# Where TensorE's operands begin within 512 bytes: the experts' and five blocks' stored values moved by some bytes

## The chip, the core and the metric

The kernel runs on one core of a Trainium2 chip. The metric is the device time of one execution in microseconds, lower is better; the median of three runs is given, and one more execution was taken with the hardware profiler.

## The reference

Two transformer blocks follow one another over 256 tokens of 1024 features, in float32. The first has four feed-forward parts, two mixers between them and norms; the second has two layers of three mixers each, one feed-forward part and one mixture of eight experts. What the change touches is the feed-forward part (five times) and the experts:

```python
def swiglu(h, w_gate, w_up, w_down):          # 1024 -> 2816 -> 1024
    return (jax.nn.silu(h @ w_gate) * (h @ w_up)) @ w_down

def moe_swiglu(h2, w_router, w_gate, w_up, w_down):
    logits = (h2 @ w_router).astype(jnp.float32)
    top_logits, top_idx = lax.top_k(logits, TOP_K)          # 2 of 8
    top_w = jax.nn.softmax(top_logits, axis=-1)
...
    hid = jax.nn.silu(lax.ragged_dot(xs, w_gate, sizes)) * lax.ragged_dot(xs, w_up, sizes)   # 1024 -> 3584
    y = lax.ragged_dot(hid, w_down, sizes)                                                    # 3584 -> 1024
```

## The kernel before, in words

Every product of a weight matrix is made of three matmuls. A number is split into a high part that the float32r type holds and the rest, and hi·hi, hi·lo and lo·hi are added up in PSUM (`mm3w`, `mm3x`; the matmul itself is line 250). Weights come from HBM as a stream of chunks of 1 MB (`raw`, line 142 on SyncE's queue). ScalarE makes the high part of two pieces of 512 columns at a time (`wh`, line 159), VectorE the rest (`wl`, line 160). Four buffers of each are in turn use, and the next pieces are loaded and split some pieces ahead.

There are two ways to multiply. In `proj_t`, used by the five feed-forward blocks, the weights are the stationary operand (128 columns of `wh` or `wl`) and the activations are streamed, 256 columns at a time. A block's first half streams `xh` and `xl` (1056 matmuls), its second half streams the block's inner values `hh` and `hl` (`ffn_core`; 22 pieces of 128 features by 4 outputs of 256 by 2 by 3, 528 matmuls). In `proj_x` and in the experts it is the other way round: the activations are stationary (128 columns) and the weights are streamed, 512 columns at a time. In `moe`, `gate_up` has the gathered tokens `gxh` and `gxl` as the stationary operand, and `down` has the hidden values `mhh` and `mhl`. `gather` fetches an expert's tokens with a one-hot matrix `P`, which is streamed against `xh` and `xl`; `scatter` streams an expert's result `yhl` against the transposed one-hot matrix `PT`.

In the profile a matmul is named out<-moving,stationary: `pa<-xh,wh` streams `xh` against loaded `wh`. PEld is the loading of the stationary operand; it runs ahead, so that one matmul streams while the next one's operand is loaded.

The blocks run in this order: block 1 (first block's layer 0, first part), the even mixer, blocks 2 and 3, the odd mixer, block 4, the first layer of mixers, block 5 (`ffn2`), the second layer of mixers, the experts.

Tiles are placed by pools, one after the other. `gap(pool, n, name)` (line 178) takes n bytes per partition of a pool and never uses them, so that what follows begins n bytes later. Every slice that a matmul reads begins at a multiple of 512 bytes within its tile, so the byte at which the tile begins, within 512, is that of all its operands. In the built program `wh` and `wl` begin at byte 448, `xh` and `xl` at 128, whatever the gaps.

Of the kernel before, what the change touches and what calls it, by code (L numbers as in the profile page):

```python
# [177 lines left out]
def gap(pool, n, name):  # L178

    pool.tile([128, n // 4], F32, name="gap_" + name)


class Net:
# [1193 lines left out]
        self.ln_finish(self.vec("lnmix", 0, 8), self.vec("lnmix", 8, 8))  # L1379

    def ffn2(self):
        self.ffn_core("ffn_w_gate_2", "ffn_w_up_2", "ffn_w_down_2", (0,), (0,), None, self.residual2, free=128)
        self.ln_finish(self.vec("lnffn", 0, 8), self.vec("lnffn", 8, 8))

    def ln_stats(self, x):
# [56 lines left out]
    def moe(self):  # L1442
        nc, tc, W = self.nc, self.tc, self.wk
        V = nc.vector
        Z = self.mo
        x = self.hx
        C = self.consts(Z, "moe")
        gap(Z, 256, "mo")
        cr = Z.tile([128, 2, 128], F32R, name="cr")
        V.tensor_copy(cr[:, 0], C["before"])  # L1450
        V.tensor_copy(cr[:, 1], self.ones)
# [296 lines left out]
    def run(self):  # L1748
        tc = self.tc
        self.setup()  # L1750
        with tc.tile_pool(name="evw", bufs=1, reuse_waits="tile") as P:
            steps = self.even_loads(P)
            self.ffn1(0, 0, steps, free=352)
            for _ in steps:
                pass
            self.even()
        with tc.tile_pool(name="s5p", bufs=1, reuse_waits="tile") as P2:
            with tc.tile_pool(name="s5q", bufs=1, reuse_waits="tile") as P:
                steps = self.s5_params(P, P2)
                self.ffn1(0, 1, steps, free=128)  # L1760
                self.ffn1(1, 0, steps, free=128)
                for _ in steps:
                    pass
            self.odd()
        self.ffn1(1, 1, after=self.between)
        self.ctx1.close()
        with tc.tile_pool(name="l2", bufs=1, reuse_waits="tile") as Q:
            self.l2 = Q
            gap(Q, 128, "l2")
            self.layer0()  # L1770
        self.ffn2()
        self.run_last()
# [100 lines left out]
```

## Time and profile before

| what | value |
|---|---|
| three runs | 3131.31, 3135.25, 3145.41 us |
| median | 3135.25 us |
| profiled execution | 3134.77 us |
| its span | 3133.0 us |
| TensorE busy in matmuls | 3042.3 us, 97% of the span |
| loading of stationary operands | 2739.8 us, 87% |
| VectorE busy | 2334.4 us, 75% |
| ScalarE busy | 1870.3 us, 60% |
| read from HBM | 691.92 MB |
| mean granted clock of TensorE | 0.989 |

A matmul's duration in the profile runs from its start to the end of its last column and overlaps the next one's, so the busy share of TensorE does not tell its pace. The pace is the time from start to start. A row of the timeline gives starts to 0.01 us (x2 stands for two merged matmuls); a row of the table of stretches gives the number of matmuls that lie in a stretch, those included that began just before it.

### The profile page before, as it was taken

To read this page: it belongs to the slowest core of one execution; us is meant where nothing else is said; L and a number is where in the kernel's file an instruction comes from. 1 tells how busy PE (TensorE), PEld (TensorE's weight loads), DVE (VectorE), ACT (ScalarE), POOL (GpSimd) and SP (SyncE) were. 2 spreads that over 40 slices of the span, in tenths; PEclk is the share of its full clock that TensorE was granted. 3 is DMA by queue.
4 is the path that set the end of the run, shared out by engine and by line. 5 is a ranking of instruction groups with operands and counts; after the bars stand their busy time and mean duration, and the time that the engine had idled before them with its cause. 6 is when DMAs were issued, how large, how long until landed. Compare 5 with 4: busy or idle time off the path is not lost. (4 is left out here: it accounts for less than half of the span.)

```text
span 3133.0 us, 51873 instructions
## 1 busy us (share of the span) xinstructions
PE 3042.3 (97%) x20841; PEld 2739.8 (87%) x20841; DVE 2334.4 (75%) x3444; ACT 1870.3 (60%) x2561; POOL 177.6 (6%) x155
## 2 busy tenths in 40 slices
PE   8999999999999999999999999999999999999998
PEld 8997999995899899899998898987787777877876
DVE  6667787868766675566556765569999888889888
ACT  5456555552453654554546654458787777777775
POOL 1000000002102000112010000000000000000000
PEclk9999999999999999999999999999999999999999
DMA  6542555551455333454553335659998998998993
GB/s 251 199 162 92 180 189 180 198 212 55 167 197 177 134 123 137 170 194 159 192 189 122 122 130 184 239 201 348 349 366 325 352 359 331 358 355 328 359 359 151
DMA packets 97415, 696.38 MB, mean 222 GB/s; under 512 B 10880, under 2 KB 11232, under 8 KB 13456
## 3 DMA queue, kind: packets, MB, share of 16 engines
q1 hardware_dynamic: 95184, 685.81, 59.5%
q0 software_dynamic: 752, 3.85, 0.4%
q8 instruction: 165, 2.70, 0.3%
q10 hardware_dynamic: 1232, 3.34, 0.3%
q14 instruction: 82, 0.67, 0.1%
HBM read 691.92 MB, written 1.05 MB: 221 GB/s over the span
## 5 line engine op out<-in xcount | busy, mean ns | idle before, releaser
L160 DVE TENSOR_TENSOR wl<-raw,wh 128x1024 fp32r<-128x1024 f32 x1299 | 1583.2, 1236 | 491.5 <-ACT wh L159 483.0
L159 ACT ACTIVATE wh<-raw 128x1024 fp32r<-128x1024 f32 x1299 | 1361.7, 1060 | 791.1 <-PE pa L250 643.7
L250 PE MATMUL pa<-xh,wh 128*128 128x256 f32 x3072 | 864.3, 281 | 12.9 <-ACT wh L159 9.5
L250 PE MATMUL pa<-xl,wh 128*128 128x256 f32 x3072 | 862.4, 281 | 4.0 <-DVE xl L348 3.9
L250 PE MATMUL pa<-xh,wl 128*128 128x256 f32 x3072 | 861.7, 281 | 1.0 <-DVE wl L160 1.0
L250 PEld LDWEIGHTS pa<-xh,wh 128*128 128x128 f32 x3072 | 582.4, 190 | 17.0 <-ACT wh L159 9.5
L250 PEld LDWEIGHTS pa<-xl,wh 128*128 128x128 f32 x3072 | 583.5, 190 | 6.4 <-DVE xl L348 5.0
L250 PEld LDWEIGHTS pa<-xh,wl 128*128 128x128 f32 x3072 | 585.0, 190 | 1.8 <-DVE wl L160 1.5
L250 PE MATMUL pa<-wl,gxh 128*128 128x512 f32 x896 | 354.5, 396 | 1.4 <-DVE wl L160 1.3
L250 PE MATMUL pa<-wh,gxl 128*128 128x512 f32 x896 | 353.9, 395 | 0.0
L250 PE MATMUL pa<-wh,gxh 128*128 128x512 f32 x896 | 322.5, 395 | 0.0
L250 PE MATMUL pa<-hh,wl 128*128 128x256 f32 x880 | 245.5, 279 | 0.0
L250 PE MATMUL pa<-hl,wh 128*128 128x256 f32 x880 | 245.5, 279 | 0.0
L250 PE MATMUL pa<-hh,wh 128*128 128x256 f32 x880 | 245.3, 279 | 0.0
L250 PEld LDWEIGHTS pa<-wl,gxh 128*128 128x128 f32 x896 | 168.1, 188 | 44.8 <-DVE wl L160 4.1
L250 PEld LDWEIGHTS pa<-wh,gxh 128*128 128x128 f32 x896 | 168.0, 188 | 40.8
L250 PEld LDWEIGHTS pa<-wh,gxl 128*128 128x128 f32 x896 | 168.1, 188 | 40.6
L250 PE MATMUL pb<-wl,mhh 128*128 128x512 f32 x448 | 179.1, 400 | 1.1 <-DVE wl L160 1.1
L250 PE MATMUL pb<-wh,mhl 128*128 128x512 f32 x448 | 177.9, 397 | 0.0
L250 PEld LDWEIGHTS pa<-hh,wl 128*128 128x128 f32 x880 | 166.0, 189 | 0.1
L250 PEld LDWEIGHTS pa<-hl,wh 128*128 128x128 f32 x880 | 165.9, 189 | 0.0
L250 PEld LDWEIGHTS pa<-hh,wh 128*128 128x128 f32 x880 | 165.8, 188 | 0.0
(508 smaller groups left out, 4040.3 us busy)
## 6 DMA issues: line engine op xcount, KB each, us to landing
raw<-in_moe SPq DMA_DIRECT2D x336, 1024.0 KB, 5.7
raw<-in_dense SPq DMA_DIRECT2D x315, 1024.0 KB, 4.8
c_lay<-in_c_lay POOLq DMA_DIRECT2D x2, 1152.0 KB, 7.0
x<-in_xt SPq DMA_DIRECT2D x4, 256.0 KB, 5.7
raw<-in_dense SPq DMA_DIRECT2D x4, 256.0 KB, 6.3
w<-in_cw ACTq DMA_DIRECT2D x1, 1024.0 KB, 8.1
out_dram<-hx SPq DMA_DIRECT2D x2, 512.0 KB, 2.6
c_odd<-in_c_odd POOLq DMA_DIRECT2D x1, 768.0 KB, 4.6
```

Source lines behind the costliest of these rows:

```text
L159: self.nc.scalar.activation(h, src, AF.Copy)
L160: self.nc.vector.tensor_sub(l, src, h)
L250: self.nc.tensor.matmul(out, l, r, start=start, stop=stop, skip_group_check=True)
```

## The change

Six sizes of gaps are altered, one argument is added, and nothing else:

```diff
     def ffn2(self):
-        self.ffn_core("ffn_w_gate_2", "ffn_w_up_2", "ffn_w_down_2", (0,), (0,), None, self.residual2, free=128)
+        self.ffn_core("ffn_w_gate_2", "ffn_w_up_2", "ffn_w_down_2", (0,), (0,), None, self.residual2, free=352)
...
         C = self.consts(Z, "moe")
-        gap(Z, 256, "mo")
+        gap(Z, 448, "mo")
...
             steps = self.even_loads(P)
-            self.ffn1(0, 0, steps, free=352)
+            self.ffn1(0, 0, steps, free=480)
...
                 steps = self.s5_params(P, P2)
-                self.ffn1(0, 1, steps, free=128)
-                self.ffn1(1, 0, steps, free=128)
+                self.ffn1(0, 1, steps, free=384)
+                self.ffn1(1, 0, steps, free=96)
...
-        self.ffn1(1, 1, after=self.between)
+        self.ffn1(1, 1, after=self.between, free=32)
```

Every engine has the same instructions in the same order with the same waits, in both built programs. What moves is where tiles begin, in the built programs' bytes per partition:

| tiles | begin before, within 512 | after, within 512 |
|---|---|---|
| `hh`, `hl` of block 1 | 141952, 128 | 142080, 256 |
| of block 2 | 179840, 128 | 180096, 384 |
| of block 3 | 179840, 128 | 179808, 96 |
| of block 4 | 123008, 128 | 123040, 160 |
| of block 5 | 122496, 128 | 122720, 352 |
| `gxh`; `gxl` has the same byte within 512 | 137472, 256 | 137664, 448 |
| `mhh`, `mhl`, first buffer of three | 153856, 256 | 154048, 448 |
| `P` of the gather | 135424, 256 | 135616, 448 |
| `PT` of the scatter, first buffer of two | 166272, 384 | 166464, 64 |

(For `hh` the first number is that of `hh`; `hl` begins 22528 bytes later, at the same byte within 512.) The small tiles of the experts' pool move by the same 192 bytes. `wh`, `wl`, `xh`, `xl`, `yhl`, the chunks and everything else stay.

## Rows read from the trace of the kernel before

**Rows 1.** Busy time of each engine in stretches, dense part, then experts.

```profile
core 0: us, PE busy (x) PEld busy (x) DVE busy (x) ACT busy (x) POOL busy (x), PEclk, DMA share, GB/s
0.00:220.00 220.00, 209.19 (x1776) 208.20 (x1776) 143.88 (x184) 108.85 (x149) 16.64 (x17) 1.00 0.60 213
220.00:440.00 220.00, 216.86 (x1758) 201.32 (x1757) 170.74 (x448) 128.86 (x260) 9.56 (x6) 0.98 0.41 145
...
2420.00:2640.00 220.00, 217.22 (x970) 174.46 (x969) 197.51 (x190) 170.62 (x192) 0.00 (x0) 1.00 0.92 350
```

**Rows 2.** Waits from 2200 to 3000 us: us in total, times, longest.

```profile
SPq L142 <- DVE wl L160: 673.0, 260, 6.8
...
ACT wh L159 <- DMA raw<-in_moe: 13.4, 40, 0.3
```

**Rows 3.** TensorE in stretches of 256-column matmuls alone: two first halves, six second.

```profile
350.00:440.00 90.00, 90.00 (x766) 1.00 0.53 189
560.00:630.00 70.00, 70.00 (x620) 1.00 0.54 189
140.00:198.00 58.00, 58.00 (x495) 1.00 0.53 183
455.00:512.00 57.00, 57.00 (x487) 1.00 0.53 187
640.00:694.00 54.00, 54.00 (x479) 1.00 0.55 195
980.00:998.00 18.00, 18.00 (x161) 1.00 0.57 180
1578.00:1590.00 12.00, 12.00 (x108) 1.00 0.55 188
1600.00:1637.00 37.00, 37.00 (x317) 1.00 0.53 186
```

**Rows 4.** Timeline of TensorE, experts: first and last of 71 starts.

```profile
2293.66 0.39 PE L250 MATMUL pb<-wh,mhh 128*128 128x512 f32 x1
...
2310.00 0.40 PE L250 MATMUL pb<-wl,mhh 128*128 128x512 f32 x1
```

**Rows 5.** The same, second layer's projections: first and last of 48 starts.

```profile
1908.24 0.39 PE L250 MATMUL pa<-wh,xh 128*128 128x512 f32 x1
...
1919.00 0.39 PE L250 MATMUL pa<-wh,xl 128*128 128x512 f32 x1
```

**Rows 6.** The same, 256 columns of weights streamed: first and last of 39.

```profile
1023.12 0.28 PE L250 MATMUL pa<-wh,xh 128*128 128x256 f32 x1
...
1027.43 0.28 PE L250 MATMUL pa<-wh,xl 128*128 128x256 f32 x1
```

**Rows 7.** The same, the gather, two places.

```profile
2348.25 0.39 PE L250 MATMUL pb<-P,xl 128*128 128x256 f32 x2
...
2348.72 0.40 PE L250 MATMUL pb<-P,xl 128*128 128x256 f32 x2
...
2349.89 0.40 PE L250 MATMUL pb<-P,xh 128*128 128x256 f32 x2
...
2350.61 0.40 PE L250 MATMUL pb<-P,xl 128*128 128x256 f32 x2
```

**Rows 8.** Groups of the page: busy us, mean ns; idle before, releaser.

```profile
L250 PE MATMUL pa<-wl,gxh 128*128 128x512 f32 x896 | 354.5, 396 | 1.4 <-DVE wl L160 1.3
...
L250 PE MATMUL pa<-hh,wl 128*128 128x256 f32 x880 | 245.5, 279 | 0.0
...
L250 PE MATMUL pb<-wl,mhh 128*128 128x512 f32 x448 | 179.1, 400 | 1.1 <-DVE wl L160 1.1
```

**Rows 9.** The experts' stage: its ends, its loads, two stretches of matmuls alone.

```profile
2104.17 0.39 PE L250 MATMUL pa<-wh,gxh 128*128 128x512 f32 x1
...
3116.14 0.40 PE L250 MATMUL pb<-wh,mhl 128*128 128x512 f32 x1
...
raw<-in_moe SPq DMA_DIRECT2D x336, 1024.0 KB, 5.7
...
2264.00:2275.00 11.00, 11.00 (x49) 1.00 1.00 375
2300.00:2308.00 8.00, 8.00 (x36) 1.00 0.98 376
```

## The prediction

> **What bounds the kernel now.** I read the table of stretches first. In the dense part TensorE is busy nearly all the time while DMA stands at 0.41 to 0.60; in the experts TensorE is again busy 217 of 220 us, but DMA stands at 0.92 [rows 1]. The queue's own waits say that the experts' loads are not late: SP waited 673 us of an 800 us stretch for a weight buffer to come free, and the split on ScalarE waited only 13.4 us for data [rows 2]. So TensorE sets the end in both parts, and what matters is its pace: the time from one matmul's start to the next one's.
>
> The pace comes from a timeline (last start less first start, over the steps between) or from a stretch that holds one kind alone (its length plus one duration of 0.28 us, over its count; a missing record or two shifts that by some tenths of a ns). For two matmuls of 256 columns the same instructions on the same bytes run at two levels. In the first block's first half 766 in 90 us are 117.9 ns each, in the third's 620 in 70 us are 113.4 ns [rows 3]. The half that the change touches has both levels too: 495 in 58 us (117.7), 487 in 57 us (117.6), 479 in 54 us (113.3), 161 in 18 us (113.5), and in the fifth block first 108 in 12 us (113.7, that is 113.3 within a record), then 317 in 37 us (117.6) [rows 3]. I call 113.3 and 117.8 the two levels and their difference, 4.4 ns, a step. The clock is granted in full (1.00, that is 2.4 GHz) in all of these.
>
> For the experts' 512 columns there are 70 steps from 2293.66 to 2310.00, 233.4 ns each [rows 4]. The same shape in another place, the second layer's projections with xh and xl as the loaded operand, makes 47 steps from 1908.24 to 1919.00, 228.9 ns each [rows 5]: one step lower.
>
> **What differs between those two places is the byte.** While one matmul streams its moving operand, the stationary operand of the next is loaded. Let D be the byte at which the loaded operand starts less that of the streamed one, within 512. In the blocks D is 448-128 = 320, in the experts 256-448, again 320; in the place of [rows 5] it is 128-448, that is 192. Two smaller places widen this. 256 columns at D = 192 make 38 steps in 1027.43-1023.12 us, 113.4 ns [rows 6]; the gather, at D = 128-256 = 384, makes 6 steps from 2349.89 to 2350.61, 120.0 ns, and elsewhere 4 from 2348.25 to 2348.72, 117.5 ns [rows 7]. So along D = 192, 320, 384 the pace stays or rises: 113.4, then 113.3 or 117.8, then 117.5 to 120.0; and 228.9, then 233.4. That is the whole evidence; no steady run at D = 0, 64, 96, 288 or 352 exists in the trace.
>
> **The change part by part.** No instruction is added, removed or moved, no DMA either, so everything hangs on 4032 expert matmuls (3 x 896 and 3 x 448) and 2640 of the blocks' second half (3 x 880) [rows 8].
>
> Experts: D goes from 320 to 0, which is 512 on a circle of 512. Seen from 384, 0 lies 128 bytes further on in the direction in which the pace rose; seen from 192 it lies 192 bytes back. I take the first, and one step only: 233.3 + 4.4 = 237.8 ns. 4032 x 4.44 ns = **+17.9 us**. Nothing hides it, as TensorE has no slack there. The other ends: one step down, the level of [rows 5], -17.9; two steps either way, 35.8.
>
> The rule that speaks against any effect is dealt with among the rivals.
>
> Blocks, 528 matmuls each, in order of time, with D after: the first (192) goes from 117.8 to the 113.4 of [rows 6], -2.3 us; the second (64, beyond 0 in the rising direction) from 117.8 to 122.2, +2.3 (by the other end -2.3); the third (352, between 320 and 384) from 113.3 to 117.8, +2.3 (or 0); the fourth (288) stays at 113.3, 0 (or +2.3); the fifth (96), now 113.3 for about a quarter and 117.8 for the rest, 116.7, goes to 122.2, +2.9 (or -1.8). Sum **+5.2 us**, ends -6.4 and +9.8.
>
> Gather and scatter: the gather's D goes from 384 to 192, some 96 of its 128 matmuls at full clock by about 6 ns, -0.6 us; the scatter's goes from 256 to 448, 64 matmuls, +0.3 by one step. Together **-0.3 us**. The other tiles that follow in the experts' pool move by 192 bytes too, but feed VectorE and ScalarE, which have slack (197 and 171 of 220 us) [rows 1], and no wait is new.
>
> The sum is 17.9 + 5.2 - 0.3 = +22.8 us on the profiled execution's 3134.8 us: **3157.6 us**, with the 0.5 us by which the median lies above it 3158. Of what is not in the sum: the first halves keep their bytes but may come to stand at the other level after another pause; that is 1056 x 4.44 ns = 4.7 us for each block, of either sign, and three such flips are about what the three runs of before spread (3131 to 3145).
>
> **Rivals.** *Faster: the rise wraps before D = 0.* What returns to its start after 512 bytes must fall somewhere, between 384 and 512 or between 512 and 704 (which is 192). If it falls before 512, the experts stand at the low end: 228.9, -17.9 us, or 224.4, -35.8. The place is the 4032 expert matmuls alone, and it decides as soon as a run of 70 shows a pace under 231 ns. With the blocks at 64 and 96 low as well (-6.4 and less) the time is 3110, or 3093 with two steps. Weights would come fast enough: the stage runs from 2104.17 to 3116.14 us, 1012 us, for 336 chunks of 1024 KB, 352.3 MB, 348 GB/s; 36 us less asks for 361, and stretches without anything else move 375 and 376 GB/s [rows 9]. For it: the share of the circle left for the fall, 320 bytes, of which 128 lie before 512. Against it: nothing between 192 and 384 shows a fall.
>
> *No change: the byte does not matter, or one level stays.* The two levels at equal bytes in [rows 3] show that something other than D sets the pace as well, and the same history could have put [rows 5] one step lower. Then the experts stay at 233.3, the blocks trade a few us and the time is 3135, give or take 7. The Trainium skill, "SBUF — State Buffer", section "Who interferes with whom", gives TensorE two independent read ports, one for the streamed operand and one for the weight load, and says that it never waits on anyone; by that rule D cannot matter and the sum would be 0. The trace agrees only in part: [rows 4] against [rows 5] differ by 4.5 ns per matmul, in dozens of steps each. That the change does not do what it says can be set aside: the built program's addresses are those named above.
>
> *Slower by more.* If the rise goes on at 4.4 ns per 128 bytes from 320, D = 512 costs a step and a half to two: up to +35.8, with the blocks' upper end +9.8, about 3180.
>
> **How the numbers follow.** No change means within 0.5%, 15.7 us, about what a measurement of this kernel can tell. Slower, one step or two: 0.48, since both shapes rise from 192 on. Faster: 0.31, since 128 of 320 bytes would be 0.4, less a little for the two-level spread that favours no step. No change: 0.21. The slower case alone holds 3150 to 3182. The range for 8 in 10 takes in the one-step faster case and its flips, 3102, and the two-step slower one, 3182.
>
> **What would show it.** Right: runs of 70 expert matmuls at 237.8 ns or more, the stage 18 us longer than 2104 to 3116, DMA below 0.92, and the blocks' second halves at 113 in the first and above 118 in the second and fifth. Wrong in the size: 242 ns. Wrong in the sign: 228.9 or less. Wrong in kind: 233.3 unchanged, or levels in the second halves that do not follow D.

## The result, and the profile after

The changed kernel takes 3117.76 us, the median of 12 runs (3104.48 to 3133.01); the kernel before, run beside it, 3138.02 (3123.37 to 3147.78). The ratio is 0.9937 with an interval of 0.9919 to 0.9956: faster by 0.6%, where the prediction said slower. The profiled execution took 3122.09 us, its span is 3120.3 us, 12.7 less than before, at the same mean granted clock of 0.989.

The page after gives the groups that answer to [rows 8] (busy us, mean ns of one | idle before, releaser), and the loads.

```profile
span 3120.3 us, 51873 instructions
...
L250 PE MATMUL pa<-wl,gxh 128*128 128x512 f32 x896 | 349.9, 390 | 1.6 <-DVE wl L160 1.4
...
L250 PE MATMUL pa<-hh,wl 128*128 128x256 f32 x880 | 247.1, 281 | 0.0
...
L250 PE MATMUL pb<-wl,mhh 128*128 128x512 f32 x448 | 177.3, 396 | 1.1 <-DVE wl L160 1.1
...
raw<-in_moe SPq DMA_DIRECT2D x336, 1024.0 KB, 5.7
```

The experts' matmuls went from 396 and 400 ns to 390 and 396, the blocks' from 279 to 281: the two parts of the change moved in opposite directions. The timeline of TensorE after gives the pace: the stage's first and last matmul, and between them the first and last of 71 starts in one run, which answer to [rows 4].

```profile
2113.87 0.39 PE L250 MATMUL pa<-wh,gxh 128*128 128x512 f32 x1
...
2282.76 0.39 PE L250 MATMUL pb<-wh,mhh 128*128 128x512 f32 x1
...
2298.66 0.39 PE L250 MATMUL pb<-wl,mhh 128*128 128x512 f32 x1
...
3103.44 0.39 PE L250 MATMUL pb<-wh,mhl 128*128 128x512 f32 x1
```

70 steps in 15.90 us are 227.1 ns, against 233.4 before. The stage lasts 3103.44 - 2113.87 = 989.6 us, against 1012.0 [rows 9]: **-22.4 us**. But it begins 9.7 us later than the 2104.17 of before. So the dense part lost **+9.7 us**, and -22.4 + 9.7 = -12.7 is the whole of the span's change. Over all its steps the stage divides like this (mean of the steps under 250 ns, and the sum of all steps of the kind):

```
                             before            after
gxh, gxl loaded (2631)   233.3 ns, 616.9 us   226.9 ns, 600.6 us   -16.3
mhh, mhl loaded (1239)   233.2 ns, 294.7 us   228.3 ns, 288.8 us    -5.9
gather, scatter and others         100.4 us            100.2 us     -0.2
```

The table of stretches after, in the places of [rows 1] and [rows 3]: two of the experts, then the second halves of the five blocks in order.

```profile
2200.00:2420.00 220.00, 216.69 (x991) 177.60 (x990) 203.08 (x198) 176.30 (x194) 0.00 (x0) 1.00 0.92 354
2420.00:2640.00 220.00, 217.17 (x991) 178.18 (x990) 201.44 (x195) 174.11 (x195) 0.00 (x0) 1.00 0.94 357
...
134.00:195.00 61.00, 61.00 (x520) 61.00 (x519) 34.04 (x34) 27.50 (x33) 2.76 (x2) 1.00 0.52 184
446.00:506.00 60.00, 60.00 (x512) 60.00 (x511) 41.59 (x67) 30.78 (x41) 2.97 (x2) 1.00 0.53 188
636.00:695.00 59.00, 59.00 (x499) 59.00 (x498) 40.53 (x67) 28.12 (x36) 3.77 (x3) 1.00 0.56 201
962.00:1004.00 42.00, 42.00 (x357) 42.00 (x356) 24.82 (x22) 18.30 (x21) 14.50 (x9) 1.00 0.52 186
1600.00:1643.00 43.00, 43.00 (x369) 43.00 (x368) 24.44 (x21) 17.57 (x18) 9.17 (x6) 1.00 0.53 183
```

In 2420 to 2640 us there are 991 matmuls where there were 970 [rows 1]. DMA went up from 0.92 to 0.94 of its time and from 350 to 357 GB/s, not down: the faster TensorE was fed. The queue's own waits from 2200 to 3000 us after:

```profile
SPq L142 <- DVE wl L160: 670.6, 265, 6.7
```

SyncE's queue still waited 670.6 us for a buffer, against 673.0 [rows 2], so the bound is the same as before.

The blocks' second halves, taken from start to start over the whole half (a stretch's length over its count comes within 1% of it):

```
block   before: D, ns    after: D, ns     said
1       320  117.8       192  117.8       113.4
2       320  117.8        64  117.8       122.2
3       320  113.3       352  118.7       117.8
4       320  113.4       288  118.3       113.3
5       320  116.6        96  117.3       122.2
```

One thing moved whose bytes did not. The place of [rows 5], 512 columns at D = 192, has its 48 starts here after:

```profile
1916.72 0.40 PE L250 MATMUL pa<-wh,xh 128*128 128x512 f32 x1
...
1927.69 0.40 PE L250 MATMUL pa<-wh,xl 128*128 128x512 f32 x1
```

47 steps in 10.97 us are 233.4 ns, where the same instructions on the same bytes took 228.9 before.

### The profile page after: what moved, and what is told of

The parts are those of the page before. It is cut to its first block, busy times and chain, and to the rows that moved or that the text cites. A ratio compares the mean times of both kernels' runs of the same rounds, so it can differ in the third digit from the quotient of the medians.

```text
span 3120.3 us, 51873 instructions
## 1 busy us (share of the span) xinstructions
PE 3029.6 (97%) x20841; PEld 2749.1 (88%) x20841; DVE 2331.8 (75%) x3444; ACT 1869.7 (60%) x2561; POOL 177.9 (6%) x155
```

## The experiments

The prediction's theory was a pace that rises with D in steps of 4.4 ns; its rivals were a fall before D = 0, and a pace that does not depend on D. Two kinds of kernels tell them apart: small ones with nothing but matmuls, and the network with one part of the change.

### m1_sweep: every D in steps of 32 bytes

The network is left out; what is left is this, for 512 columns and then 256, each with d from 0 to 480 in steps of 32, three times over:

```diff
+for i in range(STEPS):
+    g, j = divmod(i, 3)
+    st = (xh, xh, xl)[j]
+    mv = (wh, wl, wh)[j]
+    so = (g % 8) * 128 + d // 4
+    mo = (g % 4) * 256
+    nc.tensor.matmul(o, st[:, so:so + 128], mv[:, mo:mo + cols], start=i == 0, stop=i == STEPS - 1,
+                     skip_group_check=True)
```

> This kernel leaves the whole network out: it runs 60 matmuls in a row of the kernel's float32r form for each distance D = 0, 32, ..., 480 between the loaded and the streamed operand's byte, once with 512 and once with 256 columns, three times over, with a pause for an eviction between runs and no other engine busy. Theory A (the distance sets the pace, and falls back somewhere between 384 and 512): 512 columns show about 229 ns at 192, 233 at 320, 227 at 0, the same in all three repeats, with a fall between 384 and 512; 256 columns show 113 to 118 with a shape of their own. Theory B (history: the level is drawn after each pause, whatever the bytes): the same D gives different levels in the three repeats, for 512 columns as for 256. Theory C (the other engines' traffic makes the difference): all D give one pace here.

The table of stretches shows a quiet chip: no load, no VectorE, the clock granted in full. Columns as in [rows 1].

```profile
375.00:610.00 235.00, 223.27 (x964) 176.98 (x963) 0.00 (x0) 9.35 (x16) 0.00 (x0) 1.00 0.00 0
```

The timeline, in pairs the 13th and the 60th start of a run: D = 0 and 320 with 512 columns, then D = 0 and 64 with 256.

```profile
382.74 0.39 PE L58 MATMUL pa<-wh,xh 128*128 128x512 f32 x1
...
393.39 0.39 PE L58 MATMUL pa<-wh,xl 128*128 128x512 f32 x1
...
531.93 0.39 PE L58 MATMUL pa<-wh,xh 128*128 128x512 f32 x1
...
542.90 0.40 PE L58 MATMUL pa<-wh,xl 128*128 128x512 f32 x1
...
620.38 0.28 PE L58 MATMUL pa<-wh,xh 128*128 128x256 f32 x1
...
626.02 0.28 PE L58 MATMUL pa<-wh,xl 128*128 128x256 f32 x1
...
636.21 0.28 PE L58 MATMUL pa<-wh,xh 128*128 128x256 f32 x1
...
641.54 0.28 PE L58 MATMUL pa<-wh,xl 128*128 128x256 f32 x1
```

47 steps: 226.6, 233.4, 120.0 and 113.4 ns. All of it, worked out in this way:

```
D              0    32    64    96   128   160   192   224
512 columns  226.7 233.3 233.3 234.4 232.4 233.4 228.8 233.3
256 columns  120.0 118.4 113.3 117.4 118.7 120.1 113.3 116.7
```

D = 256 to 480 repeats the same row: 256 gives 226.7 and 120.0, 320 gives 233.3 and 113.3. (Two places differ between the three repeats: 256 columns came out at 117.8, 113.3 and 117.8 at 448, and at 117.7, 116.7 and 117.7 at 480. The rest agrees in all of them, the very first run at a lower clock aside.) So the circle has 256 bytes, not 512; the pace does not rise steadily along it, and at 0 the two widths stand at opposite ends: the lowest for 512 columns, nearly the highest for 256. That settles the experts: D = 0 is one of their best places, and D = 320 the same as 64.

It also settles the rival of no effect. The Trainium skill, "SBUF — State Buffer", section "Who interferes with whom", has two independent read ports for TensorE; here, with no load and no VectorE at work, the distance between the two operands alone is worth up to 7.7 ns per matmul (226.7 against 234.4). The trace does not agree with two reads that are independent.

### m2_absolute: is it D, or the byte itself?

D is held at 0, 192 and 320, and both operands move together by 0 to 448 bytes in steps of 64:

```diff
-    so = (g % 8) * 128 + d // 4
-    mo = (g % 4) * 256
+    so = (g % 8) * 128 + (d + byte) // 4
+    mo = (g % 4) * 256 + byte // 4
```

> The network is left out here too. D is held at 0, 192 and 320 while both operands move together through eight bytes, 64 apart, two repeats. If only the distance counts (theory A), the eight bytes give one pace for each D (512 columns: 227, 229, 233 ns). If the streamed operand's own byte counts, the pace goes through several levels within one D. If it is history (theory B), the two repeats of one case differ.

512 columns: 226.7 at D = 0, 228.8 at 192 and 233.4 at 320, the same at all eight bytes. 256 columns: 120.0 at D = 0 at all eight. At D = 192 all eight took 117.8, where the sweep had 113.3, and at D = 320 the first two bytes took 117.8 and the other six 113.3, alike in both repeats. At multiples of 64 bytes only D counts, but for the two levels that 256 columns have at some D, as in [rows 3].

### e1_experts_only and e2_blocks_only: the two halves of the change

```diff
-        gap(Z, 256, "mo")
+        gap(Z, 448, "mo")
```

> Only the experts' pool moves (stationary operands to the weights' byte); the five blocks stay at byte 128. Theory A: the experts' pace goes from 233.3 to 227 ns as in the whole change, 4032 x 6.2 ns = 25 us less, and the time is 3110 to 3118, the same as the whole change or a few us better; ratio 0.992 to 0.994. Rival (the blocks carry the gain through the state in which they leave TensorE): no more than a third of the gain, ratio above 0.997.

```diff
-            self.ffn1(0, 0, steps, free=352)
+            self.ffn1(0, 0, steps, free=480)
...
```

(and the other four blocks as in the change, the experts as before)

> Only the blocks' inner values move; the experts keep D = 320. Theory A: the experts stay at 233.3 ns; the second halves stand at 117 to 119 ns in all five blocks as in the changed kernel, 2640 x at most 2 ns more than before, so 0 to 6 us slower, ratio 1.000 to 1.002, not distinguishable from 1. Rival (blocks carry the gain): ratio 0.994 to 0.997.

The experts alone: 3111.1 us against 3133.9, ratio 0.992 (0.989 to 0.995). In its timeline the stage begins 0.7 us later than before, at 2104.90, and lasts 989.6 us, as in the full change.

```profile
2104.90 0.49 PE L250 MATMUL pa<-wh,gxh 128*128 128x512 f32 x1
...
3094.52 0.39 PE L250 MATMUL pb<-wh,mhl 128*128 128x512 f32 x1
```

The blocks alone: 3137.02 us, ratio 1.0016 (0.9997 to 1.0035). The table of stretches, a block's second half, then the experts:

```profile
636.00:695.00 59.00, 59.00 (x499) 59.00 (x499) 41.73 (x72) 28.85 (x37) 3.76 (x3) 1.00 0.54 190
...
2420.00:2640.00 220.00, 218.07 (x972) 175.16 (x971) 197.83 (x189) 170.71 (x191) 0.00 (x0) 1.00 0.92 349
```

The experts are at 233.3 ns again, and the five second halves at 117.8, 117.8, 118.7, 118.3 and 117.3, the same to 0.1 ns as in the full change. The gain is the experts' alone; the blocks' bytes cost 5.8 us of pace, which is too little for twelve runs to show clearly (their interval is -0.9 to +11 us).

### e3_experts_256: the period inside the network

```diff
-        gap(Z, 256, "mo")
+        gap(Z, 192, "mo")
```

(the experts' D is 256 in place of 320)

> Only the experts' pool moves, this time by 64 bytes back, to D = 256. With a period of 256 bytes the experts' pace is that of D = 0, 227 ns, and the time is 3108 to 3116, ratio 0.991 to 0.994. With a period of 512 bytes and a pace rising from 192 to 384, as the prediction had it, the pace lies between 229 and 233 ns and the time over 3118.

3105.39 us against 3125.69, ratio 0.9931 (0.9906 to 0.9956); the experts at 226.9 and 228.3 ns, the stage 989.7 us. D = 256 is D = 0. With this, five profiles have the experts at D = 0 or 256 (the change, e1, e3, and e5 and e7 below), all at 226.9 ns for `gxh` and `gxl`, and four have them at 320 (before, e2, e4 and e6), all at 233.3. A level drawn by what went before would not sort itself so.

```profile
2420.00:2640.00 220.00, 217.17 (x994) 178.25 (x993) 201.11 (x197) 173.90 (x196) 0.00 (x0) 1.00 0.93 353
```

### e4_blocks_0: the experts' best byte in the blocks

```diff
-            self.ffn1(0, 0, steps, free=352)
+            self.ffn1(0, 0, steps, free=160)
...
```

(D = 0 in the second halves of all five blocks, by free = 160, 448, 448, 320 and 448)

> Only the blocks move, all five to D = 0, where the first sweep shows 120.0 ns for 256 columns; the experts stay at 320. If the distance's effect carries over to the kernel and turns round with the shape, the second halves stand at 120.0 in all five blocks against 115.6 on the mean before: 2640 x 4.4 = 12 us slower, ratio 1.002 to 1.005. If 0 is good for every shape, the time is lower by up to 2640 x 2.3 = 6 us.

3139.9 us against 3125.69, ratio 1.0039 (1.0021 to 1.0057), and all five second halves at 119.9 to 120.0 ns. The stretches of blocks 1 and 2 (57.28 us over 478, 60.28 over 503, within two records of it):

```profile
136.00:193.00 57.00, 57.00 (x478) 57.00 (x477) 30.85 (x31) 25.48 (x30) 2.75 (x2) 1.00 0.51 186
449.00:509.00 60.00, 60.00 (x503) 60.00 (x502) 41.28 (x66) 30.26 (x40) 2.96 (x2) 1.00 0.51 185
```

What is best for 512 columns is wrong for 256, in the network as in the sweep.

### m3_fine and m6_moving_byte: below 32 bytes

```diff
-            for d in range(16):
-                out.append((cols, 32 * d))
+            for d in range(64):
+                out.append((cols, 4 * d))
```

and, with the `so` and `mo` of m2_absolute,

```diff
+        for cols, d in ((512, 0), (512, 64), (256, 64), (256, 76)):
+            for byte in range(0, 64, 4):
+                out.append((cols, d, byte))
```

> The network is left out. As the first sweep, but D in steps of 4 bytes over 256, two repeats, 48 matmuls each. The first sweep showed a period of 256 bytes, the lowest pace for 512 columns at 0 (226.7) and the highest for 256 columns at 0 and 160 (120.0 to 120.1), with two levels (113.3 and 117.8) at 64 and 192. If it is lines or banks of 32 bytes or more, the pace is flat within each 32 bytes; if it is the exact lag of two streams, it changes from one 4-byte step to the next and has levels between, perhaps under 113 for 256 columns.

D in steps of 4 bytes gives a jagged line, alike in both repeats: 512 columns lie mostly at 233.3, lowest at 0, 120, 132 and 156 (226.7), highest at 164 (237.3); 256 columns are lowest at 52, 64, 76, 88 and 180 (113.3), highest at 220 (120.8). Nothing lies below 226.7 or 113.3: D = 0 can't be beaten for the experts by D alone.

> The network is left out. The sweeps so far held the streamed operand at a multiple of 64 bytes; in the last two kernels it began 20 bytes past one, and the blocks stood at 117 and 123 ns instead of 113.3. Here D is held (0 and 64 with 512 columns, 64 and 76 with 256 columns) and both operands move together by 0, 4, ..., 60 bytes, two repeats. If the streamed operand's own byte within 64 counts, the pace changes with it at a held D, and D = 76 at 20 bytes shows 117 to 123; if only D counts, each D shows one pace for all 16 bytes, and the slow blocks of the last two kernels come from something else in the network (other beginnings, other engines).

The byte itself within 32 counts as well, with D held. Both operands move together here, so these runs do not tell whose byte it is; it is counted as the streamed one's. The timeline at D = 0, byte 20, then byte 32, each the 13th and the 48th start:

```profile
79.30 0.40 PE L58 MATMUL pa<-wh,xh 128*128 128x512 f32 x1
...
87.53 0.40 PE L58 MATMUL pa<-wh,xl 128*128 128x512 f32 x1
...
115.73 0.39 PE L58 MATMUL pa<-wh,xh 128*128 128x512 f32 x1
...
123.67 0.39 PE L58 MATMUL pa<-wh,xl 128*128 128x512 f32 x1
```

35 steps: 235.1 and 226.9 ns. The first eight bytes:

```
streamed byte           0     4     8    12    16    20    24    28
512 columns, D = 0    226.7 237.7 231.1 228.8 231.1 235.1 233.3 228.3
256 columns, D = 76   113.3 121.2 120.0 117.2 120.1 123.4 120.0 117.3
```

The next 32 bytes repeat the first row within 0.1 ns. The second row repeats but for byte 48, 116.6 against 120.1 at 16; and of 512 columns at D = 64, bytes 44 and 48 took 231.1 and 228.8 against 233.4 and 233.3 at 12 and 16, alike in both repeats. Whether the period is longer there, or these are two levels again, is open.

### m4_start and m5_start_fine: what chooses between two levels

One or three other matmuls go ahead of the same sixty of 256 columns:

```diff
+ahead = {"none": (), "short": ((n, d),), "other": ((256, n),) * 3, "wide": ((512, d),) * 3}[kind]
+for w, e in ahead:
+    nc.tensor.matmul(b[:, :w], xh[:, e // 4:e // 4 + 128], wh[:, :w], start=True, stop=True,
+                     skip_group_check=True)
```

> The network is left out. At D = 64 and 192 with 256 columns, where two levels were seen, each run of 60 is begun in 15 ways: at once, after one shorter matmul of 32 to 224 columns, after three matmuls at another D, after three of 512 columns. If the level is settled by the lag at which a run begins, some beginnings give 113.3 and others 117.8, the same in all three repeats. If it is a state of the engine that outlives pauses, or chance, the repeats of one beginning differ, or neighbours in time agree whatever the beginning.

At D = 64 the sixty matmuls run at 113.3 ns after nothing, and after one short matmul of 32, 96, 128, 160, 192 or 224 columns, but at 117.8 after one of 64; three matmuls at another D give 113.3 (0, 160, 224) or 117.8 (32, 96, 128), and three of 512 columns 117.8. Each is the same in all three repeats, where the clock was up. At D = 192 it is 117.8 after 14 of 15 beginnings. In the timeline, 47 steps after a short matmul of 32 columns (113.4 ns), then of 64 (117.7):

```profile
24.51 0.28 PE L67 MATMUL pa<-wh,xh 128*128 128x256 f32 x1
...
29.84 0.28 PE L67 MATMUL pa<-wh,xl 128*128 128x256 f32 x1
...
32.28 0.28 PE L67 MATMUL pa<-wh,xh 128*128 128x256 f32 x1
...
37.81 0.28 PE L67 MATMUL pa<-wh,xl 128*128 128x256 f32 x1
```

So the level is settled when a run begins, and over its sixty matmuls it stays. The matmuls put ahead are not the whole beginning, though: D = 192 after nothing is at 117.8 here and at 113.3 in m5_start_fine, and D = 448 and 480 of m1_sweep changed between repeats with the same matmuls before them. What else takes part is open.

> The network is left out. The fine sweep showed the low level, 113.3 ns for 256 columns, at D = 52, 64, 76, 88 and 180; here each of them, and 192, is begun in 15 ways, two repeats of 48 matmuls. If the low level at 52, 76, 88 or 180 is the only one there, it shows for all 15 beginnings, and a kernel whose activations stand at such a D would keep it after every pause: some 11900 matmuls, of which about half now stand 4.4 ns higher, 26 us. If each of them has a second level, as 64 has (117.8 after five of 15 beginnings), no choice of bytes alone keeps the low one, and what is left is to choose the one with the fewest slow beginnings.

Some D are nearly safe from it. Of 15 beginnings those above 113.3 ns were: D = 52 one, 64 five, 76 one, 88 four, 180 seven, 192 thirteen. The upper level is not the same everywhere: 120.0 at 52 and 76, 116.7 at 88.

### e5_best76 and e6_dense76: a try at the safe byte, which missed

```diff
+def pair(pool, n, name):
+    t = pool.tile([128, 2 * n * S + 8], F32R, name=name + "hl")
+    return [t[:, 5 + i * n * S:5 + (i + 1) * n * S].rearrange("p (k t) -> p k t", k=n) for i in range(2)]
...
-        self.xh = self.one.tile([128, KD, S], F32R, name="xh")
-        self.xl = self.one.tile([128, KD, S], F32R, name="xl")
+        self.xh, self.xl = pair(self.one, KD, "x")
```

(the same for `hh` and `hl`, with free = 320, 96, 96, 480 and 96, so that D is 332, which by the period is 76, in both halves of the blocks; e5 has the experts at D = 0 too)

> The experts at D = 0, and xh, xl, hh and hl at D = 76 by 20 bytes inside their tiles. If the level is settled by the beginning of a run, and 76 has the low level after 14 of 15 beginnings, the blocks' two halves and the mixers' projections stand at 113.3 to 113.6 ns nearly throughout: of 11856 matmuls those at 117.8 before (some 40 to 50%) gain 4.4 ns, 21 to 26 us, less 2 us for the 512-column matmuls against xh and xl, which go to 233.3. With the experts' 25 us that makes 3085 to 3095 us, ratio 0.984 to 0.988. Rival (the network's beginnings are others than the 15 tried, or its other engines upset the level): the blocks stand at 113 and 120 in turn, and the time is that of the experts alone, ratio 0.991 to 0.994.

> The same with the experts left at D = 320. If the two gains are independent, the ratio is 0.992 to 0.994 (19 to 24 us), and the experts stand at 233.3 ns; if the dense part has no gain at 76, the ratio is within 0.998 to 1.002.

Both lost: 3172.51 us, ratio 1.0138 (1.0110 to 1.0166), and without the experts' byte 3195.3, ratio 1.0208 (1.0183 to 1.0234). In e5 the matmuls that stream xh and xl stood at 120.0 ns in most long runs and at 123.3 in the rest, 120.8 on average. To reach D = 76 the streamed operand had been moved 20 bytes, and m6_moving_byte has 123.4 ns for just that byte; it has no 120.0 there, so the small kernel gives the direction and not the whole pace. The difference of the two medians, 22.8 us, is the experts' gain once more.

### e7_shift12: the weights moved instead

```diff
+            a = self.ring[1] * SPLIT + self.shift
...
-        self.hi_p, self.lo_p = pool("hi", 4), pool("lo", 4)
+        self.ring = [pool("whl", 1).tile([128, 8 * SPLIT + 8], F32R, name="whl"), 0]
...
-        self.ws = Stream(tc, a["dense"], (self.raw_p, self.hi_p, self.lo_p))
+        self.ws = Stream(tc, a["dense"], (self.raw_p, self.ring, 3))
```

(the dense part's `wh` and `wl` begin 3 elements, 12 bytes, in, the experts' do not; gaps chosen so that nearly all 256-column matmuls have D = 76 with the streamed byte at 0 within 32, and the experts D = 0)

> The dense stream's weights begin 12 bytes later than the experts', inside one tile that holds all buffers of wh and wl, and the blocks' and mixers' streamed values stay at a multiple of 32 bytes: D = 76 for nearly all 256-column matmuls, and D = 0 for the experts. At the start of the experts a few instructions stand in another order. If the pace is settled by D, the streamed operand's byte within 32 and the beginning, the blocks stand at 113.3 to 113.6 ns in both halves of all five (some 13400 matmuls, 115.3 to 115.8 on the mean before: 25 to 33 us) and the experts at 227 (25 us): 3075 to 3090 us, ratio 0.981 to 0.987. If something else in the network decides the level of the 256-column matmuls, they stand at two levels as before and the time is that of the experts alone, ratio 0.990 to 0.994; if D = 76 itself is bad there, as the 20-byte kernels had it, the blocks stand at 117 and 123 and the ratio is over 1.01.

3100.93 us against 3127.84, ratio 0.9918 (0.9901 to 0.9935): the lowest median of all. The table of stretches has the five second halves at 113.2 to 114.8 ns by their counts (113.3 to 113.4 from start to start; in the last two a little other work lies between), and the first halves were at 113.4 to 113.8:

```profile
136.00:193.00 57.00, 57.00 (x505) 57.00 (x504) 32.68 (x32) 26.86 (x32) 2.76 (x2) 1.00 0.53 187
441.00:498.00 57.00, 57.00 (x506) 57.00 (x505) 41.45 (x67) 30.46 (x40) 3.01 (x2) 1.00 0.52 190
624.00:681.00 57.00, 57.00 (x505) 57.00 (x505) 40.70 (x68) 28.41 (x37) 3.79 (x3) 1.00 0.55 197
926.00:983.00 57.00, 56.93 (x499) 56.63 (x498) 35.08 (x33) 26.01 (x30) 14.52 (x9) 1.00 0.54 188
1566.00:1622.00 56.00, 56.00 (x491) 55.75 (x490) 31.09 (x28) 24.10 (x25) 9.49 (x6) 1.00 0.56 189
```

All ten halves at the low level at once, which no other profile here has, agrees with the three causes: D, the streamed byte within 32, and the beginning. The time does not follow as far. One long stretch in the first layer's mixers stood at 120.0 ns, 951 matmuls from 1298.5 to 1412.6 us, where before had 113.3 throughout:

```profile
1299.00:1412.00 113.00, 113.00 (x944) 113.00 (x944) 64.08 (x68) 58.66 (x66) 15.78 (x14) 1.00 0.51 182
```

120.0 is the level that m5_start_fine found at D = 76 after one of its 15 beginnings, so D = 76 is not safe in the network. It cost about 6 us. With it counted, the paces of the dense part's 256-column matmuls still come to some 18 us less than before, but the experts began only 10.3 us earlier, at 2093.91. Ahead of the experts TensorE had a granted clock of 0.50 (1.2 GHz) for 68.3 us in place of 58.0; at 213 ns for 256 columns there, against 113.3, these 10 us are worth some 5 by estimate, and about 3 us stay open. The ratio can't be told from those of the experts alone, 0.992 and 0.9931.

## Why the prediction was wrong, point by point

**The bound: right.** TensorE sets the end, and a change of its pace alone came through in full: 22.4 us less in the stage, with DMA at 0.94 and no new wait. The prediction's D is the right variable for the experts, as e1, e3 and m2_absolute show, but not the only one: m6_moving_byte has 226.7 to 237.7 ns at one D.

**The experts' term: wrong in sign, and this decides the result.** The step that failed is "Seen from 384, 0 lies 128 bytes further on in the direction in which the pace rose". It drew the direction from two points of 512 columns, D = 192 and 320, and carried it on to 384 by [rows 7], which are of 256 columns; and it took a circle of 512 bytes for granted. The sweep shows 256 bytes, no direction at all, and opposite ends for the two widths at 0. In place of 237.8 ns the runs have 226.9 and 228.3; in place of +17.9 us, -22.4. What one could have read: for 512 columns the trace had two points, and two points say nothing about a third. Even these two are no slope: in the profile after, the place of [rows 5] stood at 233.4 with its bytes unchanged, the pace of D = 320. There the rival "No change" was right that [rows 5] may have stood at the lower of two levels; it was wrong on the experts, which stood at one pace for each D in all nine profiles.

**The rival "Faster" was right in kind, wrong in its reason and its price.** It had D = 0 at the low end, one step down (228.9) or two (224.4). The pace, 226.9, is neither: it is no multiple of the 4.4 ns step. With the blocks low as well it gave 3110; they were not low, and 3118 is what came. That 3118 lies between the prediction's 3102 and 3182 is owed to this rival, which set the lower end, and not to the term that was forecast.

**The blocks' term: the sum right, nearly all its parts wrong.** Said +5.2, measured +5.8 (528 times the differences of the table above). Block 1 was to gain 4.4 ns and gained none; 2 and 5 were to rise to 122.2 and stayed at 117.8 and 117.3; 4 was to stay and rose by 5. Only block 3 came within 1 ns of its price, and blocks 3 and 5, which have the same D by the period (352 and 96), stand at 118.7 and 117.3. The misses cancelled, which is luck, and the 5.8 itself hangs on the levels that this profile of before drew: against e1's, which has the same bytes in the blocks, it is 4.2. Behind block 1 stands [rows 6], one run of 39 matmuls at D = 192: m4_start has this D at 117.8 after 14 of 15 beginnings, so the row showed the exception. The trace of before had the other level too, at the same D and the full clock, the first and last of 21 starts:

```profile
240.39 0.28 PE L250 MATMUL pa<-wh,xh 128*128 128x256 f32 x1
...
242.75 0.28 PE L250 MATMUL pa<-wh,xl 128*128 128x256 f32 x1
```

20 steps are 118.0 ns. A single run at one of two levels was taken for the byte's own. (A slip beside it, on which nothing hangs: the 766 matmuls from 350 to 440 us are of the second block's first half, not of the first's.)

**The flips of the first halves: as said.** Block 1 came out at 113.3 in place of 117.8, 3 and 4 the other way; by pace, with the projections of x, this cost 4.6 us: one flip is left over, for which 4.7 was allowed. With the second halves' 5.8 it makes the dense part's +9.7 within 0.7. The flips can't be put down to the change: e1 and e3 have the dense part's bytes of before, and their experts began 0.7 us later and 8.7 us earlier than before; e2 has those of the change, and its experts began 6.4 us earlier than the change's.

**Gather and scatter:** said -0.3; in the sums above, all that is not expert matmuls changed by -0.2.

**What would show it.** "237.8 ns or more" was refuted by one run of 70 matmuls (227.1 ns), "the stage 18 us longer" by its two ends (22.4 us shorter), and DMA stood at 0.94, not below 0.92. The sign that was named for a theory wrong in kind came too: block 1 at 117.8 with D = 192 is a level that does not follow D.

## What to carry to other kernels

Where every float32r matmul loads a new stationary operand and TensorE is the bound, the bytes at which the two operands begin are a tuning knob worth up to 5 or 9% of a matmul from the worst place to the best (226.7 to 237.7 ns, 113.3 to 123.4), and 2 to 3% for the experts here: sweep them in a small kernel, for each width apart, since a place that is best for 512 columns may be among the worst for 256. Move tiles by whole multiples of 32 bytes unless the sweep covers the streamed byte too. And where a trace shows two levels for the same instructions at the same bytes, one run at one of them is no price.

## What the runs showed of the hardware that was not expected

- The pace of float32r matmuls with a new stationary operand each depends on D with a period of 256 bytes, and at equal D on the byte itself, with a period of 32 that does not hold at every byte: 226.7 to 237.7 ns for 512 columns, 113.3 to 123.4 for 256, in kernels of matmuls alone.
- Between neighbouring 4-byte steps of D the pace jumps by up to 6.7 ns (226.7 at 156, 233.4 at 160). What in the chip gives these numbers is open.
- Some D have two levels (256 columns: 113.3 and 117.8 at 64 and 192; 512 columns in the network: 228.9 and 233.4 at 192), and the beginning of a run chooses between them. In m4_start and m5_start_fine each beginning repeated; two places of m1_sweep did not. That these flips also make up most of what the same kernel's runs differ by (3123 to 3148 us here) fits their size, but is not shown: first halves at the same bytes stood at different levels in the profiles of before and of e3_experts_256.
- The Trainium skill, "TensorE: Matmul & The Clock Gate", section "Back-to-back issue gap", gives 512/2.4 + 2.5 = 216 ns between isolated matmuls and about 131 ns in a stream of load and matmul pairs. No run here came below 226.7 ns for 512 columns at the full granted clock, so neither is reached with these float32r operands.
